# First modulation loads of a two-layer diffusion backbone: buffers, order of the identity and of the first projection's weights

## The chip, the cores and the metric

The kernel runs on one core of one Trainium2 chip, in one launch. The metric is the device time of one execution in microseconds. The numbers of the profile come from one profiled execution; the time of a kernel is the median of several executions.

## The reference

The model has two layers over one stream of 512 tokens (256 context tokens, then 256 latent tokens) of width 1024. Each layer computes six modulation vectors of width 1024 for the latent tokens and six for the context tokens, and uses two of them (a scale and a shift) on the normalised tokens before a combined input projection. Cut to what matters here:

```python
sh1_l, sc1_l, g1_l, sh2_l, sc2_l, g2_l = split(silu(c) @ ada_w[i] + ada_b[i], 6)
sh1_c, sc1_c, g1_c, sh2_c, sc2_c, g2_c = split(silu(c_ctx) @ ada_w[i] + ada_b[i], 6)
h = rms_norm(xs, mix_norm_w[i]) * (1 + sc1) + sh1
y = token_mixer(h, ...)          # u = h @ w_in[i], three mixers, merge, output projection
xs = xs + g1 * y
h = rms_norm(xs, ffn_norm_w[i]) * (1 + sc2) + sh2
xs = xs + g2 * ffn(h)            # dense in layer 0, top-2 of 8 experts in layer 1
```

The modulation weights of a layer are a matrix of 1024 x 6144. All arithmetic is in 32 bits; the output is the final normalised latent stream.

## The kernel before, in words

Tokens are kept transposed: eight tiles of 128 channels by 512 tokens. The modulation weights of a layer are cut into 24 loads of 256 output columns, each a tile of 128 x 2048 numbers (1 MB). Loads 0 to 3 of layer 0 give the shift before the mixers and loads 4 to 7 the scale; two loads (one of each) make two of the eight channel tiles ready.

A framework orders the instructions of each engine: it takes them by program order as priority, moves what is written under a high priority mark ahead, and lets an instruction go when its inputs and its buffer are free; what an engine runs is then a fixed order. Buffers come from pools. A pool that is opened inside a `with` gives its memory back at the end, and what is put there next waits for the last readers of it.

The start of the program does this:

- Small loads, then the eight token tiles (lines 235 to 243), all on SP's queue.
- `Norm.add` squares each tile on ScalarE (line 452) and adds on VectorE (454); two matmuls with a matrix of constants sum over channels (465, 466); the root is taken on ScalarE (424, 425). VectorE multiplies each tile by it (line 902, eight times).
- Four modulation tiles are loaded into the two 32 KB buffers `hlo` and `hhi`, two in each (line 907), then the identity matrix, the first 128 columns of the constants (line 909).
- A loop goes over the eight modulation loads in the order 4, 0, 5, 1, 6, 2, 7, 3. At its fifth step (`PLAN["pre"]` is 4) the first tile of the input projection's weights is loaded by `load`. `ada` multiplies a modulation tile with the conditioning vectors (line 373, sixteen matmul instructions a tile), copies the result (376) and gives back its own ending, `ada_end`, which is called after the next `ada`: it transposes with the identity (392), reduces (394), adds the bias (400) and, for a scale, forms a coefficient (404).
- Tiles five to eight take `load` as well (line 337): a counter `turn["raw"]` picks one of three buffers of 8 KB in `wpool`, which the projection's weights use too. In later stages the same counter chooses between `wpool` and further buffers: modulo 7 in the feed-forward layer, modulo 10 in the expert stage, where three places of the ten (`PLAN["slots"]`) are halves of `hhi` and `hlo`.
- The rest of the constants and the masks are loaded (917, 918).
- `modulate` scales and shifts each channel tile on VectorE (481) and splits it into a high part on ScalarE (482) and a low part on VectorE (483), written to `hhi` and `hlo`.
- `mixers` opens with memory of a pool of its own, `mix0`. It walks over 29 weight tiles in a written order; the first two are `("cx", 1)` and `("v", 0)`. Before the work of a tile, `filler` puts in the loads and products of further modulation tiles. `project` splits weights into high and low parts under the high priority mark (`split`, lines 346 and 347; two halves of a tile, each 128 x 1024) and runs 24 matmuls a half (353 to 355). `lru` convolves its result: a first tap on ScalarE (665), three on VectorE (671), also under the mark, and then loads a small matrix `l_bd` on ScalarE's queue (673). `values` splits the weights of `v` (346, 347) and multiplies (545 to 547). The scores' tiles `h_sc` and `h_sf` are cleared by GpSimd (578, 580).
- Much later, after the output projection of layer 0, the feed-forward layer begins: its first loads are two weight tiles and one tile of layer 1's modulations, which is summed row-wise on VectorE (line 385) with conditioning vectors `rc` that are broadcast by a load on ScalarE's queue (946) and passed through ScalarE (949).

The product of a high and a low part with high and low weights is:

```python
T.matmul(ps, whi(k), hhi(k), ...)
T.matmul(ps, whi(k), hlo(k), ...)
T.matmul(ps, wlo(k), hhi(k), ...)
```

Of the kernel before, what the change touches and what calls it, by code (L numbers as in the profile page):

```python
# [11 lines left out]
F32 = mybir.dt.float32  # L12
# [7 lines left out]
P = 128  # L20
# [61 lines left out]
def host_layout(x, c, ctx, c_ctx, ada_w, ada_b, mix_norm_w, ffn_norm_w, w_in, hg_lb_logits, hg_norm_w,  # L82
# [89 lines left out]
PLAN = {  # L172
    "moe": (4, 1),
    "ps": (3, 3, 1, 1),
    "ffn": (4, 0),
    "mix": ((0, 0), (0, 1)),
    "fa": 11,
    "pre": 4,
    "hold": 5,
    "ff": (1, 1),  # L180
    "sg": 1,
# [15 lines left out]
def tile_kernel(ctx: ExitStack, tc: tile.TileContext, xT, cT, cR, ada_w, w_in, w_br, w_out, ffn_gu, ffn_d, router,  # L197
                moe, lru_bd, vec, cst, lmask, outT, dbg=None):
    nc = tc.nc
# [8 lines left out]
    hpool = ctx.enter_context(tc.tile_pool(name="hpool", bufs=1))  # L208
# [6 lines left out]
    def nm(s):  # L215
        cnt[0] += 1
        return f"{s}_{cnt[0]}"
# [9 lines left out]
    def pm(shape=(P, 512)):  # L227
        return pt("pm", n_pm, shape)
# [92 lines left out]
    def take(kind, base):  # L321

        turn[kind] += 1
        own = more["own"] if kind == "raw" else []
        return wpool if turn[kind] % (base + more[kind] + len(own)) < base else more["pool"]

    def load(ap, n=2048):
        if more["own"]:
            j = turn["raw"] % (3 + more["raw"] + len(more["own"]))
            if j in PLAN["slots"]:  # L330
                turn["raw"] += 1
                r = more["own"][PLAN["slots"].index(j)]
                nc.sync.dma_start(r[:, :n], ap)
                return r
        p = take("raw", 3)
        r = p.tile([P, 2048], F32, tag="raw", name=nm("raw"), bufs=3 if p is wpool else more["raw"])
        nc.sync.dma_start(r[:, :n], ap)
        return r
# [26 lines left out]
    def ada(i, n, raw=None):  # L365

        if raw is None:
            raw = load(ada_w[i, n])
        raw = raw.rearrange("p (k c) -> p k c", k=KD)
        ps = pm()  # L370
        for k in range(KD):
            g = k % 4
            T.matmul(ps[32 * g:32 * g + 32, :256], csil[:, k, :], raw[:, k], start=k < 4, stop=k >= 4,  # L373
                     tile_position=(0, 32 * g))
        a = tpool.tile([P, 256], F32, tag="ada", name=nm("ada"), bufs=2)
        V.tensor_copy(a, ps[:, :256])
        return lambda: ada_end(i, n, a)
# [11 lines left out]
    def ada_end(i, n, a):  # L389
        pp = pm((P, 2, P))  # L390
        for q in range(2):
            T.transpose(pp[:, q], a[:, q * P:(q + 1) * P], ident)
        o = mods[i][:, 2 * n:2 * n + 2]
        V.tensor_reduce(o, pp.rearrange("p q (g r) -> p q r g", r=32)[:, :, 0:2], AX.X, ALU.add)
        ada_bias(i, n, o)
# [11 lines left out]
    pending, early, ends, on_rows = [], [], [], []  # L407
# [492 lines left out]
        norm.add(xts[k])  # L900
    for k in range(KD):
        V.tensor_tensor(xts[k], xts[k], norm.r, ALU.mult)
    first, raws = [4, 0, 5, 1, 6, 2, 7, 3], []
    for k, tg in ((0, "hlo"), (2, "hhi")):
        raw = hpool.tile([P, 2, 2048], F32, tag=tg, name=nm("ada0"))
        for q in range(2):
            nc.sync.dma_start(raw[:, q], ada_w[0, first[k + q]])
            raws.append(raw[:, q])
    nc.sync.dma_start(cc[:, :C_BD], cst[:, :C_BD])
    end = lambda: None  # L910
    for k, n in enumerate(first):
        if k == PLAN["pre"]:
            early.append(load(w_in[0, 0]))
        end, done = ada(0, n, raws[k] if k < 4 else None), end
        done()
    end()
    nc.sync.dma_start(cc[:, C_BD:], cst[:, C_BD:NCST])
    nc.sync.dma_start(lm, lmask)
    pending += [(0, n) for n in range(8, 24) if n not in PLAN["dv"][0]]
# [19 lines left out]
    with tc.tile_pool(name="ffn", bufs=1) as fp:  # L939
# [11 lines left out]
        for hf in range(2):  # L951
# [18 lines left out]
            for m in range(KD):  # L970
                raw = load(ffn_d[hf, m], 11 * P)
# [351 lines left out]
    for pr in range(4):  # L1323
        st = {}
# [18 lines left out]
    with tc.If(n_most > 0):  # L1343
        for e in range(NE):
# [6 lines left out]
            for k in range(KD):  # L1351
                pg = pm()
                for n, (s_, t) in enumerate(PARTS):
                    T.matmul(pg[:, :P], hn[s_][:, t, k * P:(k + 1) * P].bitcast(F32), oh[:, t],
                             start=n == 0, stop=n == 3)
# [11 lines left out]
            for g in range(6):  # L1367
# [3 lines left out]
                for u in range(2):  # L1371
                    ps = pj()
                    for c in range(8 // kc):
                        n = 4 * g + 2 * u + c if g < 5 else 20 + u
                        raw = load(moe[e, n]).rearrange("p (k c) -> p k c", k=kc)
# [12 lines left out]
            for c in range(11):  # L1388
                raw = load(moe[e, 22 + c]).rearrange("p (k c) -> p k c", k=4)
                for k in range(4):  # L1390
                    h_, kk = DOWN[4 * c + k]
                    first, last = (kk == 0, kk == 21) if h_ == 0 else (kk == 20, kk == 19)
# [52 lines left out]
```

## Time and profile before

| what | value |
|---|---|
| time, median of 3 runs | 2145.86 us (2144.93 to 2146.93) |
| profiled execution, its own time | 2144.67 us |
| its span, first to last instruction | 2142.8 us |
| TensorE busy | 2049.2 us, 96% |
| VectorE busy | 1304.7 us, 61% |
| ScalarE busy | 928.2 us, 43% |
| mean granted TensorE clock | 0.985 of full speed |
| read from memory | 452.01 MB, 211 GB/s over the span |

Busy time is the time in which an engine has at least one instruction under way. A granted clock of 1.00 is 2.4 GHz and one of 0.50 is 1.2 GHz; a stretch with both shows a mean between them. Times in the trace count from the start of the span. SPq and ACTq are the instruction streams of SyncE and ScalarE where they issue a transfer; such a row has the time of issue, and the table of DMA issues has the time from issue to landing.

### The profile page before, as it was taken

The numbers are of one execution on the slowest core, as the hardware profiler recorded it, in microseconds if no ns is written. First come the engines' busy times: TensorE is split into PE (matmuls) and PEld (weight loads), VectorE is DVE, ScalarE is ACT, GpSimd is POOL, SyncE is SP. The second block draws the span as 40 slices with busy tenths as digits, with TensorE's granted clock in tenths as the row PEclk, the third lists the DMA queues.
The fourth block names the chain that finished last, engine by engine and source line by source line (L and its number), as shares of the span: only waits on it lengthen the run. The fifth ranks groups of instructions, "written<-read, shape, count | busy, mean of one in ns | idle before, by whom it ended". The sixth has DMA issues, their size and how long they took to land.

```text
span 2142.8 us, 34452 instructions
## 1 busy us (share of the span) xinstructions
PE 2049.2 (96%) x13828; PEld 1578.5 (74%) x13828; DVE 1304.7 (61%) x2363; ACT 928.2 (43%) x1427; POOL 35.3 (2%) x101
## 2 busy tenths in 40 slices
PE   6999999999989999999999999989999999999997
PEld 3777777777868878887778888878757856865863
DVE  6667457764455468634777777669618707915941
ACT  3653234323334222223755443348527616715831
POOL 0001000000000000000000000000000000000000
PEclk9999999999999999999999999989999999999999
DMA  8341423112262346322333222369999999999996
GB/s 322 107 168 70 158 79 118 41 61 79 103 250 98 132 162 250 137 68 81 113 122 119 99 104 93 142 240 351 369 421 421 381 419 418 370 398 420 378 382 257
DMA packets 66984, 455.36 MB, mean 213 GB/s; under 512 B 7681, under 2 KB 8193, under 8 KB 13953
## 3 DMA queue, kind: packets, MB, share of 16 engines
q1 hardware_dynamic: 64080, 447.58, 54.3%
q10 hardware_dynamic: 2736, 5.51, 0.8%
q8 instruction: 111, 1.82, 0.3%
q14 instruction: 57, 0.46, 0.1%
HBM read 452.01 MB, written 1.05 MB: 211 GB/s over the span
## 4 chain that ended last, share of the span: by engine, by line
PE 89%; DVE 4%; ACT 4%; DMA 2%; issue 1%; SPq 0%; DVEq 0%; ACTq 0%
PE pj L353 15%; PE pj L354 15%; PE pj L355 15%; PE pj L1253 7%; PE pm L1289 4%; PE pm L1234 2%; PE pm L1232 2%; PE pm L1233 2%; PE pj L1196 2%; PE pj L1197 2%; PE pj L1198 2%; PE pm L590 1%; PE pa L798 1%; PE pm L373 1%; PE po L1198 1%
## 5 line engine op out<-in xcount | busy, mean ns | idle before, releaser
L346 ACT ACTIVATE whi<-raw 128x1024 fp32r<-128x1024 f32 (+3 forms) x442 | 436.1, 993 | 563.6 <-PE pj L354 480.3
L347 DVE TENSOR_TENSOR wlo<-raw,whi 128x1024 fp32r<-128x1024 f32 (+3 forms) x442 | 497.6, 1140 | 207.4 <-ACT whi L346 196.9
L353 PE MATMUL pj<-hhi,whi 128*128 128x512 f32 (+1 forms) x1216 | 452.3, 373 | 11.0 <-ACT hhi L482 8.5
L355 PE MATMUL pj<-hhi,wlo 128*128 128x512 f32 (+1 forms) x1216 | 450.6, 371 | 0.4 <-DVE wlo L347 0.4
L354 PE MATMUL pj<-hlo,whi 128*128 128x512 f32 (+1 forms) x1216 | 449.6, 370 | 0.1
L353 PEld LDWEIGHTS pj<-hhi,whi 128*128 128x128 f32 x1216 | 231.3, 190 | 52.4 <-ACT hhi L482 11.6
L354 PEld LDWEIGHTS pj<-hlo,whi 128*128 128x128 f32 x1216 | 231.2, 190 | 38.4 <-issue 2.3
L355 PEld LDWEIGHTS pj<-hhi,wlo 128*128 128x128 f32 x1216 | 230.9, 190 | 37.9 <-issue 2.5
L1253 PE MATMUL pj<-raw,whole 128*64 128x256 f32 (+1 forms) x1088 | 114.4, 362 | 0.0
L1260 DVE TENSOR_TENSOR act<-act,pj 128x256 f32<-128x256 f32 (+1 forms) x24 | 9.6, 399 | 156.6 <-ACT act L1259 156.6
L1253 PEld LDWEIGHTS pj<-raw,whole 128*64 128x64 f32 x1088 | 73.6, 137 | 33.1 <-issue 2.5
L1259 ACT ACTIVATE act<-pj 128x256 f32<-128x256 f32 (+1 forms) x24 | 8.8, 366 | 144.3 <-PE pj L1253 144.3
L353 PE MATMUL pj<-yhi,whi 128*128 128x512 f32 (+1 forms) x192 | 66.7, 350 | 3.4 <-ACT yhi L508 3.1
L355 PE MATMUL pj<-ahi,wlo 128*128 128x512 f32 x176 | 69.2, 393 | 0.8 <-DVE wlo L347 0.8
L353 PE MATMUL pj<-ahi,whi 128*128 128x512 f32 x176 | 69.1, 393 | 0.0
L1232 PE MATMUL pm<-whi,ahi 128*128 128x512 f32 x176 | 69.0, 392 | 0.0
L1197 PE MATMUL pj<-whi,xg 128*128 128x512 f32 (+1 forms) x192 | 68.8, 359 | 0.0
L1233 PE MATMUL pm<-whi,alo 128*128 128x512 f32 x176 | 68.6, 390 | 0.0
L354 PE MATMUL pj<-alo,whi 128*128 128x512 f32 x176 | 68.5, 389 | 0.0
L1196 PE MATMUL pj<-whi,xg 128*128 128x512 f32 (+1 forms) x192 | 68.4, 356 | 0.1
L1234 PE MATMUL pm<-wlo,ahi 128*128 128x512 f32 x176 | 68.2, 390 | 0.0
L1198 PE MATMUL pj<-wlo,xg 128*128 128x512 f32 (+1 forms) x192 | 68.1, 354 | 0.0
(364 smaller groups left out, 3613.8 us busy)
## 6 DMA issues: line engine op xcount, KB each, us to landing
raw<-in_moe_dram SPq DMA_DIRECT2D x185, 1024.0 KB, 8.8
raw<-in_w_in_dram SPq DMA_DIRECT2D x58, 1024.0 KB, 4.9
own<-in_moe_dram SPq DMA_DIRECT2D x53, 1024.0 KB, 9.0
raw<-in_ada_w_dram SPq DMA_DIRECT2D x44, 1024.0 KB, 5.0
whole<-in_moe_dram SPq DMA_DIRECT2D x26, 1024.0 KB, 8.6
raw<-in_ffn_gu_dram SPq DMA_DIRECT2D x22, 1024.0 KB, 4.8
raw<-in_w_br_dram SPq DMA_DIRECT2D x12, 1024.0 KB, 4.9
raw<-in_ffn_d_dram SPq DMA_DIRECT2D x16, 704.0 KB, 4.1
```

What stands on the lines that cost most here:

```text
L346: S.activation(hi, src, AF.Copy)
L347: V.tensor_tensor(lo, src, hi.bitcast(F32), ALU.subtract)
L353: T.matmul(ps, whi(k), hhi(k), start=first and k == 0, stop=False)
L354: T.matmul(ps, whi(k), hlo(k), start=False, stop=False)
L355: T.matmul(ps, wlo(k), hhi(k), start=False, stop=last and k == n - 1)
L1196: T.matmul(ps[:, :w], xv[0][:, kk], hi[:, k], start=kk == 0, stop=False)
L1197: T.matmul(ps[:, :w], xv[1][:, kk], hi[:, k], start=False, stop=False)
L1198: T.matmul(ps[:, :w], xv[0][:, kk], lo[:, k], start=False, stop=kk == 7)
L1232: T.matmul(pd[h_], ahi, hi[:, k % 2], start=first, stop=False)
L1233: T.matmul(pd[h_], alo, hi[:, k % 2], start=False, stop=False)
L1234: T.matmul(pd[h_], ahi, lo[:, k % 2], start=False, stop=last)
L1253: T.matmul(ps[64 * h_:64 * h_ + 64, u, :hw], xs[:, kk], raw[:, k, h_ * hw:(h_ + 1) * hw], start=u + kk == 0, stop=u == 1 and kk == 7, tile ...
```

## The change

The first eight modulation loads get eight buffers of 8 KB per partition each, in a pool `start` that is opened and closed before the mixers' pool is opened. All loads are issued in one loop, the identity first; the first weights of the input projection go out ahead of the third modulation tile, so as the third 1 MB load (`PLAN["pre"]` is 2). A second loop does the products. `hhi` and `hlo` are no longer used for modulation tiles, and four loads fewer pass through `load` and its counter.

```diff
-    "pre": 4,
+    "pre": 2,
...
-    first, raws = [4, 0, 5, 1, 6, 2, 7, 3], []
-    for k, tg in ((0, "hlo"), (2, "hhi")):
-        raw = hpool.tile([P, 2, 2048], F32, tag=tg, name=nm("ada0"))
-        for q in range(2):
-            nc.sync.dma_start(raw[:, q], ada_w[0, first[k + q]])
-            raws.append(raw[:, q])
+
+    first = [4, 0, 5, 1, 6, 2, 7, 3]
     nc.sync.dma_start(cc[:, :C_BD], cst[:, :C_BD])
-    end = lambda: None
-    for k, n in enumerate(first):
-        if k == PLAN["pre"]:
-            early.append(load(w_in[0, 0]))
-        end, done = ada(0, n, raws[k] if k < 4 else None), end
-        done()
-    end()
+    with tc.tile_pool(name="start", bufs=1) as st:
+        raws = []
+        for k, n in enumerate(first):
+            if k == PLAN["pre"]:
+                early.append(load(w_in[0, 0]))
+            raws.append(st.tile([P, 2048], F32, tag=f"ada{k}", name=nm("ada0")))
+            nc.sync.dma_start(raws[-1], ada_w[0, n])
+        end = lambda: None
+        for k, n in enumerate(first):
+            end, done = ada(0, n, raws[k]), end
+            done()
+        end()
```

## Rows read from the trace of the kernel before

**Rows 1.** The page's busy time, share of the span and instructions of each engine

```profile
PE 2049.2 (96%) x13828; PEld 1578.5 (74%) x13828; DVE 1304.7 (61%) x2363; ACT 928.2 (43%) x1427; POOL 35.3 (2%) x101
```

**Rows 2.** Busy time by stretch: length, each engine, granted clock, DMA share, GB/s

```profile
18.40:23.31 4.91, 1.82 (x30) 0.62 (x18) 4.91 (x10) 0.00 (x0) 0.00 (x0) 1.00 1.03 424
30.00:36.00 6.00, 5.34 (x48) 2.90 (x46) 4.14 (x14) 1.89 (x3) 0.00 (x0) 1.00 0.94 389
46.00:50.10 4.10, 1.52 (x8) 0.81 (x6) 3.37 (x5) 3.33 (x4) 0.00 (x0) 1.00 0.69 254
50.10:60.00 9.90, 9.90 (x50) 7.99 (x51) 4.41 (x6) 3.86 (x6) 0.00 (x0) 0.83 0.30 106
60.00:560.00 500.00, 497.45 (x4167) 373.25 (x4166) 310.09 (x685) 198.75 (x340) 17.51 (x45) 1.00 0.27 97
```

**Rows 3.** DMA issues, one each: KB, us to landing; ada_w rows: at 6.66, 28.19, 28.80

```profile
l_bd<-in_lru_bd_dram ACTq DMA_DIRECT2D x1, 256.0 KB, 2.8
ada<-in_ada_w_dram SPq DMA_DIRECT2D x1, 1024.0 KB, 7.4
cc<-in_cst_dram SPq DMA_DIRECT2D x1, 64.0 KB, 12.5
raw<-in_w_in_dram SPq DMA_DIRECT2D x1, 1024.0 KB, 14.3
raw<-in_ada_w_dram SPq DMA_DIRECT2D x1, 1024.0 KB, 6.5
raw<-in_ada_w_dram SPq DMA_DIRECT2D x1, 1024.0 KB, 8.4
```

**Rows 4.** Timeline of SP: start us, us, then line, transfer and count

```profile
6.66 2.29 SPq L907 DMA_DIRECT2D ada<-in_ada_w_dram  x4
9.30 0.33 SPq L909 DMA_DIRECT2D cc<-in_cst_dram  x1
9.99 0.33 SPq L337 DMA_DIRECT2D raw<-in_w_in_dram  x1
28.19 1.57 SPq L337 DMA_DIRECT2D raw<-in_ada_w_dram  x2
28.80 0.96 SPq L337 DMA_DIRECT2D raw<-in_ada_w_dram  x1
```

**Rows 5.** Timeline of VectorE, 18 to 44 us

```profile
18.41 4.91 DVE L902 TENSOR_TENSOR x<-x,rstd 128x512 f32<-128x512 f32 x8
...
25.81 2.35 DVE L347 TENSOR_TENSOR wlo<-raw,whi 128x1024 fp32r<-128x1024 f32 x2
...
42.47 1.34 DVE L483 TENSOR_TENSOR hlo<-x,hhi 128x512 fp32r<-128x512 f32 x2
```

**Rows 6.** Timeline of TensorE, 27 to 50 us

```profile
27.01 0.73 PE L353 MATMUL pj<-hhi,whi 128*128 128x512 f32 x2
...
38.24 1.07 PE L373 MATMUL pm<-raw,csil 128*32 128x256 f32 x16
...
46.60 0.39 PE L355 MATMUL pj<-hhi,wlo 128*128 128x512 f32 x1
48.81 0.39 PE L545 MATMUL pj<-whi,hhi 128*128 128x256 f32 x1 [1.81 <-ACT whi L346]
```

**Rows 7.** Timeline of ScalarE, 24 to 50 us; in brackets idle before, and what ended it

```profile
24.29 2.00 ACT L346 ACTIVATE whi<-raw 128x1024 fp32r<-128x1024 f32 x2 [5.91 <-DMA raw<-in_w_in_dram]
...
47.03 0.78 ACT L665 ACTIVATE l_z<-pj,vv 128x512 f32<-128x512 f32 x1 [0.36 <-PE pj L355]
47.71 1.99 ACT L346 ACTIVATE whi<-raw 128x1024 fp32r<-128x1024 f32 x2
```

**Rows 8.** Timelines of ScalarE, VectorE and TensorE at the feed-forward layer's first loads

```profile
612.06 1.92 ACT L949 ACTIVATE rc<-rc 128x2048 f32<-128x2048 f32 x1 [8.12 <-DMA rc<-in_cR_dram]
...
614.08 1.23 DVE L385 SCALAR_TENSOR_TENSOR scr<-raw,rc 128x1024 f32<-128x1024 f32 x1 [8.92 <-ACT rc L949]
614.98 0.50 PE L353 MATMUL pj<-mhi,whi 128*128 128x512 f32 x1 [1.73 <-ACT whi L346]
...
616.89 0.50 PE L355 MATMUL pj<-mhi,wlo 128*128 128x512 f32 x1 [1.19 <-DVE wlo L347]
```

## The prediction

> **What bounds the kernel now.** I read the page's table of busy time first: TensorE is busy for 96% of the span, so only time in which it stands still, or runs at the lower of its two clocks, can be won [rows 1]. Next came the table of stretches, to find where that time lies near the edit. From 60 to 560 us TensorE is busy 497.45 of 500.00 us, so the mixers of the first layer run on it, and what is won before 60 us is carried on [rows 2]. Ahead of 60 us it isn't the bound: it works 1.82 of 4.91 us while VectorE is full (18.40 to 23.31), loses 0.66 us in 30 to 36 and 2.58 us in 46.00 to 50.10. From 50.10 to 60.00 the granted clock is 0.83 on average; with levels of 1.0 and 0.5 that is 0.17 * 9.9 * 2 = 3.4 us at 1.2 GHz, and half of it, 1.7 us, is lost [rows 2].
>
> What holds TensorE there I took from the DMA issues and SP's timeline. Issue plus time to landing gives: first modulation tile 6.66 + 7.4 = 14.1, identity 9.30 + 12.5 = 21.8, first projection weights 9.99 + 14.3 = 24.3, the last two modulation tiles 28.19 + 6.5 = 34.7 and 28.80 + 8.4 = 37.2 [rows 3, 4]. The last two differ by 2.5 us: that is the price of one 1 MB tile in a full queue. They are late because their buffers are those of the projection weights: VectorE ends its second pass over those weights at 25.81 + 2.35 = 28.16 [rows 5], and SP issues the load at 28.19 [rows 4]. The product with the last modulations runs at 38.24, the first projection ends at 46.60 + 0.39 = 46.99, and the product of the values starts at 48.81, after 1.81 us for ScalarE's high part [rows 6]. ScalarE was at the convolution's first tap of both halves before (second one at 47.03, the high part at 47.71) [rows 7].
>
> **The change, part by part.**
>
> *Loads.* Nothing is added: the same nine tiles of 1 MB and the identity go out on SP in another order, and none of the eight waits for a buffer. Starting from 14.1, with the 64 KB identity ahead (0.2 us by the 2.5 us per MB) and 2.5 us a tile, landings become: identity about 12, tiles 14.3 and 16.8, weights 19.3, the other six tiles 21.8, 24.3, 26.8, 29.3, 31.8, 34.3. So the weights come 5.0 us earlier, the last tile 2.9 us earlier, and the third and fourth tiles 2.5 us later than the 19.1 and 21.6 they have by the same step now. On SP, the rest of the constants, the masks and the next two loads stand behind the last tile, as now, but no longer wait for matmuls: their queue is full, so they land at about 38.4 (ninth modulations) and 40.9 (values' weights, by 2.5 us a tile and 1.6 us for 640 KB). A cost of the order is in the next part.
>
> *The pool.* The eight buffers lie where the mixers' buffers will lie, so the mixers' first tiles must wait for the last modulation product, at about 35. Two things that now run at the start wait with them: POOL's clearing of the score tiles, which only the heads' recurrences need, well after the values, and the 256 KB load on ScalarE's queue that lands 2.8 us after its issue at the head [rows 3]. Its absence lets the tokens in earlier: 256 KB by 2.5 us per MB is 0.6 us; bounds 0 and 0.6, and I take 0.5, nearer the price of a full queue since the tokens follow at once. Behind its issue on ScalarE stand the high copies of the last rows, which wait for the same product, so the wait costs nothing; without that cover it would be the time by which it is placed too early in ScalarE's order, up to the 7 us from 28 to 35. I keep that end for the slow side only in part, since TensorE could do the modulation products meanwhile.
>
> *VectorE.* The eight row products take 18.41 to 23.32, and the two passes over the weights come after, 25.81 to 28.16 [rows 5]. These passes have priority, and with weights at 19.3 and a first high part (1.0 us, half of the 2.00 us for two) at 20.3 [rows 7] they now cut in among the row products. Everything after the products moves by 2.35 us. From the products' end to the first projection matmul is now 27.01 - 23.32 = 3.7 us [rows 6]. Bounds for the new start: 27.01 (all 2.35 absorbed) and 29.4 (none); I take 28.6, since ScalarE's two high parts at 24.29 to 26.29, which stand ahead of the first row's copy now, are gone. Minus 0.5 from the tokens: 28.1, or 1.1 us later than now.
>
> *TensorE.* From that start everything it needs arrives faster than it can work: the fifth tile's product (1.07 us) [rows 6] falls before the start instead of behind it, minus 1.0. The idle 0.66 + 2.58 = 3.24 us closes if the first half of the projection runs ahead of the second, so that its convolution and the values' high part are done beside the second half. Sum: 3.24 - 1.1 + 1.0 = 3.1 us. Without the stop at 47 to 50 the low clock that follows it goes too: 1.7 us. Leftover waits: between 0 and 2.58 us (the stop whole); I take 0.5, nearer zero, as the weights have then lain there for 4 us. Net 4.3 us.
>
> *The clock.* Rows first: TensorE does 1.82 of 4.91 us before the start, and after a stop of 2.58 us the clock is low [rows 2]. The Trainium skill, "TensorE: Matmul & The Clock Gate", section "HAM oscillation — how this bites in real kernels", says that an array that waits for data between bursts falls back to its slow clock, so that each burst begins slow. This speaks against the change, which lengthens the thin stretch; by the rule the sum would be 2.6 us. It is a rival below.
>
> *Counters.* Four loads fewer pass through the shared counter that picks buffers. At the feed-forward layer this moves the first three loads from new buffers into those still held by the output projection. They are wanted only after the norm that follows that projection, so nothing there. But the third is a row-wise modulation tile, four VectorE passes of 1.23 us, which now come at 614.08 in front of a low part that TensorE waits for (1.19 us) behind a ScalarE that stood 8.12 us for a broadcast load [rows 8]. Bounds: minus 1.2 (that wait goes) and plus 2.5 (two of the passes land in front of the norm's products); I take 0, the two being about equal. In the experts' ring of ten the starting place shifts; all ten are filled before the first is used, so nothing; without that cover one tile, 2.5 us.
>
> The profiled execution took 2144.67 us; 2144.67 - 4.3 = 2140.4. It lies 1.2 us under the median of the three runs, 2145.86, so against the median I say **2141.6**.
>
> **The rivals.** A measurement of this kernel can tell about 0.2%, 4.3 us, from no change.
>
> *The stop stays.* ScalarE's order keeps the second convolution tap ahead of the values' high part, as at 47.03 and 47.71 [rows 7]. Then 2.58 and the clock's 1.7 aren't won: 3.1 - 2.58 = 0.5, or 2145.4. For it: both carry the same priority mark. Against: the halves should no longer end together, and the weights land before them.
>
> *The start runs slow.* A stretch of 3.4 us at half clock falls on the first matmuls: 4.3 - 1.7 = 2.6, or 2143.3. For it: the start comes later, after little work. Against: rows show the low stretch only behind a full stop.
>
> *Weights third costs what it displaces (slower).* VectorE's 2.35 us is never made up: the last low part, now ending at 42.47 + 1.34 = 43.81 [rows 5], ends 2.35 - 0.5 = 1.9 us later, the stop at the values stays behind it, and one more low stretch adds 1.7: 2145.86 + 3.6 = 2149.5; with the 2.5 us at the feed-forward layer up to 2152.0. It decides from the point where that low part ends after 43.8. Against: VectorE idles 6.00 - 4.14 = 1.86 us in 30 to 36 alone [rows 2].
>
> *The feed-forward layer wins too.* With another order of loads the broadcast comes earlier and both waits around 613 to 617 go, 1.73 + 1.19 = 2.9 [rows 8]: 2141.6 - 2.9 = 2138.7, or 2137.0 if a low stretch of 1.7 follows that stop too. For it: one load fewer in front. Against: as many buffers are free as before.
>
> *It doesn't do what it says.* The eight loads are held back by something else in the pool's place, or the order of issue stays: 2145.9.
>
> **How the numbers follow.** Forecast 0.45, the stop stays 0.20, slow start 0.08, slower 0.11, feed-forward too 0.13, no effect 0.03. The forecast's own range is 2139.9 (no leftover waits and the bound of minus 1.2) to 2143.7 (leftover 2.6), and two thirds of it lie over 4.3 us faster, as the counters' and the leftover's better ends add: 0.31, with 0.13 faster 0.44. Same: 0.14 + 0.20 + 0.08 + 0.03 = 0.45. Slower 0.11. The range goes from 2137.0 (both waits and a low stretch gone) to 2147.0 (the stop stays, and 1.6 of the 2.5 us at the feed-forward layer), which leaves out most of the slow case.
>
> **What would show it.** Right: weights landing near 19, the last modulations near 34; first projection matmul near 28 and ending by 45 to 46; values' product without a stop, full clock from 46 to 60. Wrong: the first matmul after 29.4, a stop of over 1 us before the values, a low clock after it, or a difference that arises at 600 us or in the experts, which I price at nothing.

## The result, and the profile after

The changed kernel takes 2165.03 us (median of 6 runs, 2161.72 to 2167.62) against 2145.39 us for the kernel before (6 runs beside it): a ratio of 1.0096, interval 1.0086 to 1.0106, so 19.6 us slower. I had forecast 2141.6 us. The profiled execution took 2165.19 us. Its page's busy time answers to [rows 1], and the table of stretches to [rows 2]; the stretch 800 to 850 us is new here.

```profile
PE 2052.9 (95%) x13828; PEld 1580.9 (73%) x13828; DVE 1304.6 (60%) x2363; ACT 929.0 (43%) x1427; POOL 35.4 (2%) x101
```

```profile
18.40:23.31 4.91, 1.45 (x18) 0.50 (x16) 4.91 (x8) 2.00 (x2) 0.00 (x0) 0.93 1.02 425
30.00:36.00 6.00, 6.00 (x52) 3.68 (x51) 4.83 (x14) 1.66 (x3) 0.00 (x0) 1.00 1.02 414
46.00:50.10 4.10, 2.67 (x20) 1.54 (x12) 2.13 (x4) 2.18 (x3) 0.00 (x0) 1.00 0.57 208
50.10:60.00 9.90, 8.77 (x50) 6.65 (x51) 6.07 (x8) 5.13 (x8) 0.00 (x0) 1.00 0.35 128
60.00:560.00 500.00, 497.40 (x4167) 373.33 (x4167) 309.83 (x685) 198.90 (x340) 17.50 (x45) 1.00 0.27 97
...
800.00:850.00 50.00, 39.12 (x160) 31.18 (x159) 39.46 (x71) 8.36 (x10) 0.00 (x0) 0.86 0.63 227
```

The kernel before, in that last stretch:

```profile
800.00:850.00 50.00, 49.20 (x216) 40.16 (x215) 44.66 (x78) 12.35 (x15) 0.00 (x0) 1.00 0.65 237
```

To see where the time goes I took each matmul's start in the changed kernel less the start of the same matmul before (same line, same number in its line), and the median of these over a stretch: 0.2 us at 60 to 80 us, 0.2 at 560 to 600, 3.5 at 700 to 780, **16.2 at 870 to 900**, 19.1 at the end. So nothing is won or lost at the edit by 60 us in this execution, and most of the loss lies in the feed-forward layer, where TensorE works 39.12 of 50 us instead of 49.20, and at a granted clock of 0.86. The last 2.9 us (16.2 to 19.1) arise later, and no run here explains them.

**The start.** The tiles came near to the forecast. VectorE, TensorE and ScalarE of the changed kernel at the rows that answer to [rows 5 to 7]:

```profile
17.78 3.10 DVE L902 TENSOR_TENSOR x<-x,rstd 128x512 f32<-128x512 f32 x5
20.80 2.36 DVE L347 TENSOR_TENSOR wlo<-raw,whi 128x1024 fp32r<-128x1024 f32 x2
23.07 1.89 DVE L902 TENSOR_TENSOR x<-x,rstd 128x512 f32<-128x512 f32 x3
...
44.12 1.34 DVE L483 TENSOR_TENSOR hlo<-x,hhi 128x512 fp32r<-128x512 f32 x2
```

```profile
28.18 1.20 PE L353 MATMUL pj<-hhi,whi 128*128 128x512 f32 x2
...
36.75 1.07 PE L373 MATMUL pm<-ada,csil 128*32 128x256 f32 x16
...
48.27 0.40 PE L355 MATMUL pj<-hhi,wlo 128*128 128x512 f32 x1
50.48 0.39 PE L545 MATMUL pj<-whi,hhi 128*128 128x256 f32 x1 [1.81 <-ACT whi L346]
```

```profile
48.70 0.78 ACT L665 ACTIVATE l_z<-pj,vv 128x512 f32<-128x512 f32 x1 [0.38 <-PE pj L355]
49.38 1.99 ACT L346 ACTIVATE whi<-raw 128x1024 fp32r<-128x1024 f32 x2
```

The weights' low part does cut in among the row products. The last channel's low part ends at 45.46 instead of 43.81 us, the projection at 48.67 instead of 46.99, and the stop before the values is as long as before (1.81 us), behind the same second tap on ScalarE. What evens it out is the clock: 1.00 from 50.1 to 60 us instead of 0.83.

**The feed-forward layer.** TensorE's waits from 780 to 830 us in the changed kernel, then ScalarE's and SP's timelines there:

```profile
PE pj L353 <- ACT whi L346: 10.2, 1, 10.2
```

```profile
828.10 1.47 ACT L346 ACTIVATE whi<-raw 128x768 fp32r<-128x768 f32 x2 [16.33 <-DMA raw<-in_ffn_d_dram]
```

```profile
824.02 0.33 SPq L337 DMA_DIRECT2D raw<-in_ffn_d_dram  x1
```

What held the issue of that load, the eighth load of the down projection to go out, is in SP's own waits from 817 to 826 us:

```profile
SPq L337 <- DVE raw L385: 5.5, 1, 5.5
SPq L337 <- DMA raw<-in_ada_w_dram: 1.8, 1, 1.8
```

In the kernel before, the eighth load was issued at 809.39 us; SP's waits from 806 to 811 us:

```profile
SPq L337 <- DVE wlo L347: 3.6, 1, 3.6
SPq L337 <- DMA raw<-in_ada_w_dram: 0.9, 1, 0.9
```

Before, the tile takes a buffer that the last low part of another weight tile gives free. Now it takes one that a row-summed modulation tile holds, and VectorE is behind with those sums. The buffers' addresses in the two programs say the same: the load is the down projection's seventh tile; before, it follows the sixth tile in its buffer, and in the changed kernel a row-summed tile stands between the two. The chain of waits in the changed kernel shows the whole way (start, us, what): the row-summed tile is itself loaded late, then summed in four passes, then the weights are sent for.

```profile
812.97 0.75 DVE wlo L347
813.71 0.02 issue
813.73 4.78 DMA raw<-in_ada_w_dram
818.51 0.02 issue
818.53 1.23 DVE scr L385 x2
819.77 0.40 DVE x L876
820.17 1.14 DVE raw L385 x2
821.31 1.15 DVE scr L385 x2
822.45 0.40 DVE x L876
822.85 1.14 DVE raw L385 x2
```

TensorE stands still for 10.2 us. The granted clock of 0.86 over the 50 us is 2 * 0.14 * 50 = 14 us at 1.2 GHz, but the clock falls while TensorE stands still, and only what is left of it behind the stop costs time:

```profile
829.00:843.00 14.00, 13.33 (x47) 10.34 (x48) 8.90 (x16) 2.15 (x3) 0.00 (x0) 0.78 0.63 231
```

That is 2 * 0.22 * 14 = 6.2 us, of which half, 3.1 us, is lost. With the stop it makes 13.3 us, near the 16.2 - 3.5 = 12.7 us by which the matmuls fall back here.

### The profile page after: what moved, and what is told of

Same layout as the page of the kernel before. It is cut to its first block, busy times and chain, and to the rows that moved or that the text cites. A ratio compares the mean times of both kernels' runs of the same rounds, so it can differ in the third digit from the quotient of the medians.

```text
span 2163.4 us, 34454 instructions
## 1 busy us (share of the span) xinstructions
PE 2052.9 (95%) x13828; PEld 1580.9 (73%) x13828; DVE 1304.6 (60%) x2363; ACT 929.0 (43%) x1427; POOL 35.4 (2%) x101
## 4 chain that ended last, share of the span: by engine, by line
PE 62%; DVE 4%; ACT 3%; issue 1%; DMA 1%; DVEq 0%; ACTq 0%
PE pj L353 9%; PE pj L355 9%; PE pj L354 9%; PE pj L1254 7%; PE pm L1290 4%; PE pm L1235 2%; PE pm L1234 2%; PE pm L1233 2%; PE pj L1197 2%; PE pj L1198 2%; PE pj L1199 2%; PE po L1199 1%; PE po L1197 1%; PE po L1198 1%; DVE wlo L347 1%
## 5 line engine op out<-in xcount | busy, mean ns | idle before, releaser
L353 PE MATMUL pj<-ahi,whi 128*128 128x512 f32 x176 | 70.2, 399 | 10.2 <-ACT whi L346 10.2
```

The source lines that it names most:

```text
L353: T.matmul(ps, whi(k), hhi(k), start=first and k == 0, stop=False)
```

## The experiments

By the code, the first load of the feed-forward layer is the counter's number 60 in the kernel before and number 56 in the changed one. Counted modulo seven that is place 4 and place 0 of its ring. In the expert stage, modulo ten, the counter starts from 0 and from 6.

**1. The counter alone.** Four kernels: the changed one with the four turns given back; before with four taken away; the changed one with fourteen added (modulo seven as changed, modulo ten as before); and the first with the weights fifth again, as before (`"pre": 4`). The line is the same in all, with 4, -4, 14 and 4.

```diff
+    turn["raw"] += 4
     nc.sync.dma_start(cc[:, C_BD:], cst[:, C_BD:NCST])
```

> The changed kernel, with the shared buffer counter set forward by the four loads that no longer pass through it. Theory A (the counter): the feed-forward layer then takes the same buffers for the same loads as before, the two losses there (3.3 us near 615 and 12.8 us near 815) are gone, and the start is even (plus 0.2 us at 64 us): 2145 to 2148 us, within 0.2% of before. Theory B (the moved start itself, which changes what the scheduler does later): the losses stay, 2161 to 2168 us.

> The kernel before, start untouched, with only the shared buffer counter set back by four after the first loads. Theory A (the counter): the loss appears without any change of the start, 2160 to 2168 us, with the same two steps at the feed-forward layer. Theory B (the moved start): no loss, 2143 to 2148 us.

> The changed kernel with the counter set forward by 14: its place modulo 7 (feed-forward layer) is that of the changed kernel, its place modulo 10 (expert stage) that of the kernel before. Theory A1 (the place in the feed-forward layer's ring of seven decides): the loss stays, 2160 to 2166 us. Theory A2 (the place in the experts' ring of ten decides): 2145 to 2149 us.

> The changed kernel with the counter set forward by four and the first projection's weights fifth again instead of third. Theory C (weights third push VectorE's row products and the third and fourth modulations back, which eats what the buffers won): the first projection starts near 27.0 instead of 28.2 us and ends 2 to 4 us earlier than the 48.7 us of the changed kernel, 2141 to 2145 us. Rival D (the order of products on TensorE and VectorE sets the pace, whenever the tiles land): the projection ends within 1 us of 48.7, 2145 to 2148 us.

Measured: 2150.93 (1.0022, 1.0009 to 1.0034), 2160.72 (1.0073, 1.0055 to 1.0091), 2162.45 (1.0074, 1.0050 to 1.0097) and 2150.08 (1.0021, 1.0010 to 1.0032). The first two and the changed kernel make a square: place 0 instead of place 4 costs 0.0073 with the old start and 0.0096 - 0.0022 = 0.0074 with the new one, some 16 us either way. It needs no new start, and it goes by the ring of seven and not by the ring of ten, since adding fourteen brings nothing back that stands clear of the intervals. The buffers' addresses agree: in the first kernel each of the layer's 57 loads follows the same load in its buffer as in the kernel before, in the second and third the same as in the changed kernel, and between the two sorts 34 of the 57 differ. The kernel before at place 0 shows the same stop, in TensorE's waits from 780 to 830 us and SP's from 814 to 823:

```profile
PE pj L353 <- ACT whi L346: 9.5, 1, 9.5
```

```profile
SPq L337 <- DVE raw L385: 5.5, 1, 5.5
```

With the four turns given back, some 5 us (0.0022) are left that have to do with the start; the first kernel's theory A, that the start is even, missed them. Having the weights third or fifth makes no difference to them: both theories for the fourth kernel named shorter times, and its projection ends at 49.35 + 0.39 = 49.74 us, not earlier than with the weights third.

**2. Another ring.** The changed kernel with three further buffers in that layer instead of four.

```diff
-    "ffn": (4, 0),
+    "ffn": (3, 0),
```

> The changed kernel with three instead of four further buffers in the feed-forward layer, so a ring of six. In a ring of seven, where down-projection tiles and row-summed modulation tiles alternate, each down-projection tile takes over the buffer of a row-summed tile; in a ring of six it takes over that of another down-projection tile. Theory A (the eighth down-projection tile waits for VectorE's row sums): the stop of 10.2 us at 820 and the 13.7 us of low clock behind it go, about 12 to 15 us, so 2150 to 2153, less what a smaller ring costs elsewhere (one tile of 2.5 us or two). Rival (that stop belongs to the shifted order of row sums itself, whichever buffer they hold): a stop of about the same size stays, 2162 to 2168.

2146.47 us (1.0007, 0.9997 to 1.0016): the stop is gone (TensorE is busy for all of 800 to 850 us), and the time was better than I expected. The premise of that expectation, that in a ring of six a weight tile always follows a weight tile, is wrong though, as run 4 shows: SP waits for a row sum here as well, before the eighth load (799 to 805 us), only early enough. By the addresses it is the same row-summed tile ahead of the same weight tile as in the changed kernel.

```profile
SPq L337 <- DVE raw L385: 5.6, 1, 5.6
```

**3. The start.** With the four turns given back: VectorE's and TensorE's order written by pairs of channels (two row products, two modulation products with their endings, the modulated pair, then the next); and ten matmuls of no use in the thin stretch. Then the kernel before with the identity first and nothing else.

```diff
-    for k in range(KD):
-        V.tensor_tensor(xts[k], xts[k], norm.r, ALU.mult)
...
+            if k % 2:
+                end(); end = lambda: None
+                mod_pair(k // 2)
+                if k < 7:
+                    rows(k // 2 + 1)
```

```diff
+    for q in range(10):
+        T.matmul(dps[:, :256], oned, norm_r0[:, :256], start=True, stop=True)
```

```diff
+    nc.sync.dma_start(cc[:, :C_BD], cst[:, :C_BD])
     first, raws = [4, 0, 5, 1, 6, 2, 7, 3], []
...
-    nc.sync.dma_start(cc[:, :C_BD], cst[:, :C_BD])
```

> The changed kernel with the counter moved back by four turns, and VectorE's and TensorE's order at the start written by pairs of channel tiles: two row products, two modulation products with their endings, the modulated pair, then the next two row products. Theory S (the start is held by VectorE's eight row products and by the second tile's ending behind the third tile's product): first projection matmul near 25.8 instead of 28.6, the projection's end 2 to 3 us earlier, and a shorter low clock before it: 2144 to 2148 against 2150.9. Rival (the last landing at 35.9 and TensorE's own work after it set the end): no change at 52 us, 2149 to 2152.

> The changed kernel with the counter moved back by four turns, and ten matmuls of 128x256 with no use put into TensorE's order between the second and the third modulation product, about 19 to 23.5 us, where it stands still (4.5 us of work by 0.45 us each). Theory K (the 5 us that are left with the counter moved back are the low clock after the thin stretch): the low stretch from 21 us goes or falls to 3.4 us, the mean clock of a run rises from 0.983 towards 0.985, time 2146 to 2148.5. Rival (what is left comes from waits, not from the clock): 2150 to 2153, or up to 2 us more where the matmuls get in the way of the products.

> The kernel before with the identity ahead of its first four modulation loads and nothing else (counter, buffers and the place of the weights as before). If the identity's early landing is what thins TensorE's work and lengthens the low clock: about 2150, low clock of 6.8 to 10.2 us from 21 us. If it takes away the 3.1 us wait for the identity at 21.9 and no more: 2143 to 2145. If the buffers do it and not the identity: 2145.8.

By pairs: 2150.67 us (1.0026, 1.0013 to 1.0039), no gain over 2150.93. The first projection matmul comes 4.0 us earlier than in the first kernel of run 1 (28.59), and yet the projection ends later than there (49.30 + 0.40 = 49.70), at 50.22 + 0.39 = 50.61:

```profile
24.59 1.22 PE L353 MATMUL pj<-hhi,whi 128*128 128x512 f32 x2 [2.55 <-ACT hhi L913]
...
44.58 0.73 PE L353 MATMUL pj<-hhi,whi 128*128 128x512 f32 x2 [1.90 <-ACT hhi L913]
...
50.22 0.39 PE L355 MATMUL pj<-hhi,wlo 128*128 128x512 f32 x1
```

TensorE now waits for the last pair's modulated tokens at 44.58 instead. So the first matmul is not what sets the end of this stretch; theory S fell, and the time is the one that its rival gave.

Busy TensorE: 2148.99 us (1.0018, 1.0008 to 1.0029). Its granted clock at 18 to 28 and 28 to 36 us, and below the same two stretches of the kernel that it is made from:

```profile
18.00:28.00 10.00, 8.10 (x64) 5.42 (x60) 9.91 (x23) 2.63 (x3) 0.00 (x0) 1.00 1.01 421
28.00:36.00 8.00, 8.00 (x68) 4.87 (x71) 5.44 (x18) 1.89 (x3) 0.00 (x0) 1.00 1.02 414
```

```profile
18.00:28.00 10.00, 5.19 (x50) 1.89 (x40) 9.63 (x21) 2.33 (x3) 0.00 (x0) 0.65 1.01 420
28.00:36.00 8.00, 7.99 (x56) 4.65 (x53) 5.51 (x16) 2.20 (x4) 0.00 (x0) 0.80 1.02 414
```

The low clock is gone (it was 2 * 0.35 * 10 + 2 * 0.20 * 8 = 10.2 us), and the projection ends at 47.39 us, 1.3 us ahead of the changed kernel. But by 60 to 80 us the matmuls stand 0.2 us behind those of before: the stop at the values is the same, and a low clock of 3.4 us follows it again. The interval overlaps that without the matmuls. Identity first: 2148.7 us (1.0018, 1.0006 to 1.0030). It takes away the 3.1 us wait for the identity, but TensorE then waits 3.32 us for VectorE's copy until 23.08 us, and nothing is gained; the interval lies above 1, and the time hits none of the three expectations.

**4. The start alone, with the rings alike.** Before with a ring of six; the changed kernel with the four turns given back and a ring of six (both at place 0); the changed kernel with a ring of six and the ten matmuls; and before with four turns taken away and a ring of six (both at place 2, as in run 2).

> The kernel before with three instead of four further buffers in the feed-forward layer, so a ring of six; the start as before. Theory A with the gain of the ring of six seen in the changed kernel (about 3 us from 600 to 820 us against the kernel before): the stops there shrink here too, 2141 to 2143.5. Rival (the ring of six only mends what the moved counter broke): 2145 to 2147.

> The changed kernel with the counter moved back by four turns and a ring of six in the feed-forward layer, so that all places in the rings are those of the kernel before with a ring of six; the two then differ by the start alone. Theory (the new start itself costs 3 to 5 us, most of it low clock after the thin stretch): 3 to 5 us over that kernel, 2145 to 2148. Rival (the start costs nothing, and the 5 us of the changed kernel with the counter moved back came from the feed-forward layer's first broadcast): equal to it within 1 us.

> The changed kernel with a ring of six in the feed-forward layer and the ten matmuls of no use at the start. If the low clock after the thin stretch is what the start costs: 2 us under the changed kernel with a ring of six (2146.5), so 2143.5 to 2145, and full clock from 18 to 46 us. If not: 2146 to 2148.

> The kernel before with the counter set to the changed kernel's place (minus four) and a ring of six in the feed-forward layer: all places in the rings are those of the changed kernel with a ring of six, the start is that of before. If the new start costs 2 to 5 us on the chip: 2141 to 2144, under both kernels, as the profile of the changed kernel with a ring of six is 4.9 us quicker between 38 and 813 us than that of before. If the start costs nothing: 2145.5 to 2147, as the changed kernel with a ring of six.

Measured: 2154.15 (1.0039, 1.0027 to 1.0051), 2156.32 (1.0042, 1.0029 to 1.0054), 2147.27 (1.0005, 0.9996 to 1.0014) and 2145.18 (0.9996, 0.9987 to 1.0005). The first misses both theories: at place 0 of a ring of six the stop comes back in a kernel whose start was not touched. TensorE's waits from 780 to 830 us and SP's from 807 to 812 us:

```profile
PE pj L353 <- ACT whi L346: 8.3, 1, 8.3
```

```profile
SPq L337 <- DVE raw L385: 4.7, 1, 4.7
```

So it isn't the length of the ring, it is which load meets which buffer, and, as run 2 shows, whether the row sum in it is done by then. The second kernel is 2.2 us over the first with intervals that overlap, and the fourth is 0.0011 under the changed kernel of run 2 likewise, so neither decides between its theories. The ten matmuls bring nothing here either, and no version beats the kernel before by what can be measured.

**5. Row sums off the ring.** Both kernels with three buffers of their own for the row-summed tiles and a ring of four for the weights, which puts both at the same place.

```diff
-        raw = load(ada_w[i, n]).rearrange("p (q k) -> p q k", q=2)
+        raw = more["pool"].tile([P, 2048], F32, tag="rows", name=nm("rows"), bufs=3)
+        nc.sync.dma_start(raw, ada_w[i, n])
...
-    "ffn": (4, 0),
+    "ffn": (1, 0),
```

> The changed kernel, in which the row-summed modulation tiles of the feed-forward layer have three buffers of their own and the weights a ring of four (three and one), memory as before. Theory A (a weight tile waits for the buffer that a row-summed tile holds, and which one is decided by the place in the ring): the stop of 10.2 us at 820 goes and no weight load is issued at the end of a row sum; 2147 to 2153, the shorter ring for weights costing up to two tiles of 2.5 us. Rival (VectorE's late row sums stop TensorE in another way): a stop of 8 to 10 us stays, 2158 to 2166.

> The kernel before with the same two rings, whose place is then that of the changed kernel with two rings. If the start costs 2 to 5 us: that much under it, 2144 to 2149. If the whole loss came from the rings: equal to it within 1 us.

2166.23 (1.0100, 1.0082 to 1.0118) and 2166.21 us (1.0098, 1.0084 to 1.0111): both theories miss on the size. By the addresses no weight load follows a row-summed tile any more, and the stop of 10.2 us is down to 4.2, but some 12 us are lost from 611 to 668 us already, in both. VectorE at 630 to 785 us in the changed kernel with its own row buffers, and before:

```profile
L387 DVE SCALAR_TENSOR_TENSOR rows<-rows,rc 128x1024 f32<-128x1024 f32 x27 | 33.0, 1222 | 0.2
L387 DVE SCALAR_TENSOR_TENSOR scr<-rows,rc 128x1024 f32<-128x1024 f32 x27 | 32.9, 1220 | 0.0
```

```profile
L385 DVE SCALAR_TENSOR_TENSOR scr<-raw,rc 128x1024 f32<-128x1024 f32 x7 | 8.6, 1222 | 1.8 <-DMA raw<-in_ada_w_dram 1.8
L385 DVE SCALAR_TENSOR_TENSOR raw<-raw,rc 128x1024 f32<-128x1024 f32 x6 | 7.3, 1224 | 0.2
```

54 passes there instead of 13. The shared ring had also paced the row sums; without it they bunch up early, and the weights have a ring of four instead of a share in one of seven. In the stretch 640 to 672 us VectorE has no time left, first in the changed kernel with its own row buffers, then before:

```profile
640.00:672.00 32.00, 21.45 (x69) 14.83 (x70) 31.97 (x60) 18.11 (x31) 0.00 (x0) 0.79 0.42 149
```

```profile
640.00:672.00 32.00, 29.57 (x116) 23.45 (x117) 22.31 (x33) 18.53 (x32) 0.00 (x0) 0.89 0.34 125
```

This points to the bunched sums, but how the 12 us divide between the two these runs don't tell. The pair shows no difference between the two starts; by the code, though, the experts' rings of the two begin at different places (1 and 5).

## Why the prediction was wrong

**Counters: the step that failed.** I took the term as 0, with bounds of minus 1.2 and plus 2.5, because I looked only at the layer's first three loads, where the new buffers differ, and argued that these are wanted late. Measured by itself it is 0.0073, 15.7 us (run 1). A shift of the counter does not end with the loads at which it arises: it changes the assignment of loads to buffers for the rest of the stage, so that 34 of the layer's 57 loads wait for another load's buffer than before. The rows of before had the case: row-summed tiles and weights shared one ring there, and a row sum takes four passes of 1.23 us [rows 8]. I priced one meeting of the two, at the layer's first loads, and not the later ones. Nor is it their number that counts: by the addresses a weight tile follows a row-summed tile 13 times before and 11 times in the changed kernel. One of the 11 comes too late, and TensorE stands still for 10.2 us. The first broadcast, on which my bounds rested, did go the bad way as well in this execution (ScalarE waits 10.69 us for it instead of 8.12 [rows 8], and 3.3 us are lost there), but the same loss is there with the counter given back and is not there in the kernel before at place 0; so it is not the counter's.

**Ring of ten: nothing.** Right, as far as run 1's third kernel shows: giving back that place alone does not help.

**Loads.** Right, but for the last tile: weights land at 8.94 + 10.4 = 19.3 us (forecast 19.3), the last modulations at 14.35 + 21.4 = 35.8 (34.3, and "near 34"). One reading of before was wrong without harm: only the seventh tile waited for the buffer of the projection weights; the eighth, issued at 28.80, took that of the fifth tile, whose product ended at 27.67 + 1.07 = 28.74.

**VectorE and the start.** The first projection matmul was forecast for 28.1 us and came at 28.18, with the low parts among the row products.

**TensorE: 3.1 us forecast, nothing found.** The 0.66 us at 30 to 36 went as said. The 1.0 us for the fifth tile's product did not come: it ran at 30.53 us, behind the projection's start as before. The 2.58 us at the values stayed whole (1.81 and 0.76 again), with ScalarE's second tap still ahead of the values' high part and the two halves of the projection still ending together; so the rival *the stop stays* was right about this step. And the projection ended 1.7 us later, not earlier: the seventh modulation tile landed at 12.03 + 20.2 = 32.2 us, but its product stands behind projection matmuls in TensorE's order and ran at 36.75 (before, 34.80). The sixth tile's ending comes behind that product, so VectorE was at that pair's channels until 41.4, and the eighth tile's copy began at 41.33, 1.4 us after its product. An early landing doesn't help where the order ahead of its use is fixed.

**The clock.** From 18 to 36 us it was low for 2 * 0.27 * 10 + 2 * 0.09 * 8 = 6.8 us instead of 3.4 (0.83 over 10 us before), in line with TensorE's thinner work there (4.50 of 10 us against 6.43); so the rival *the start runs slow*, which I gave 0.08, held as a mechanism. The Trainium skill, "TensorE: Matmul & The Clock Gate", section "HAM oscillation — how this bites in real kernels", says that an array waiting for data between bursts starts each burst on its slow clock; the 6.8 us agree with it. The rows that I read leave out 23.31 to 30 us, so I had missed the 3.4 us that the kernel before has there. What I did not see either is the other side: the stop before the values was not followed by a low clock in this execution, though it was as long, so the two cancel.

**The rival on the slow side** named weights third, VectorE's 2.35 us never made up and the stop staying, with the last low part near 45.7: it ended at 45.46, and the rival's 2149.5 us is close to the 2150.9 of the kernel with the counter given back. But its cause fell: with the weights fifth it is 2150.1.

**What stays open.** Five pairs of kernels differ in the start alone, the rings alike: 1.0022 against 1; 1.0096 against 1.0073; 1.0042 against 1.0039; 1.0007 against 0.9996; 1.0100 against 1.0098. The mean of the five differences is 0.0012, 2.6 us, and three of them are within what can't be told from zero; in the last pair the experts' rings are not alike. In four of the six profiles with the change's own start the matmuls at 60 to 80 us stand within 0.6 us of before (-0.1, 0.2, 0.3, 0.6), in the others 0.8 and 3.8 behind; runs of one kernel spread over up to 12 us. How often the bad start happens, and how much of the 2.6 us is it and how much the broadcast at 611 us, I could not separate. A ring of eight, which does not fit beside the other pools, and a third pair of split buffers for the mixers, which could end the stop at the values, were not tried. The 2.9 us that the changed kernel loses behind the feed-forward layer stay open too.

## What to carry to other kernels

A counter that deals buffers out to loads of different kinds is part of the schedule: when a change adds or removes loads ahead of it, list what each load of every later ring now takes over, and from which engine's work, above all where a slow reader and the bound engine's operands share the ring. Before crediting an earlier landing, ask whether the order behind it is fixed and what stands ahead of its use. And a change at one end of a program that is tied to another only through a counter is cheap to separate: give the turns back, and take them away from the kernel before.

## What the runs showed that I had not expected

- A shift of four in one counter is worth 0.0073 of 2146 us (1.0055 to 1.0091) with not one instruction of the start changed.
- Filling TensorE's thin stretch took the low clock away from 18 to 36 us (granted 1.00 instead of 0.65 and 0.80), but another low stretch came after the next stop of 1.81 us, as in the kernel before. In the changed kernel, where the thin stretch had been slow for 6.8 us, the same stop was followed by none. This is no rule: with the counter given back the clock was low for 10.2 us at the start and again behind that stop (0.66 from 50.1 to 60 us).
- The broadcast of 1 MB on ScalarE's queue landed from 9.6 to 13.7 us after its issue in the six kernels that have a ring of seven at place 4 and so the same loads in the same order around it; ScalarE, which has everything behind it in its order, stood still for 6.83 to 10.92 us of that.
